# Two feed-forward layers on one core: two output quarters of a Strassen product start from values that ScalarE and VectorE wrote into PSUM, a bank is set aside for one of them, and three gate/up pairs of a layer stay plain, where four did

## The chip, the core and the metric

The kernel runs on 1 core of a Trainium2 chip. The metric is the device time of one execution in microseconds (us). The engines are TensorE (PE, the matrix products; its weight loads are listed apart as PEld), VectorE (DVE), ScalarE (ACT), GpSimd (POOL) and SyncE (SP, which here only issues DMAs). Products go to PSUM, which has 8 banks of 512 fp32 values in each of 128 partitions; everything else lies in SBUF.

## What is computed

Two layers on x of 512 tokens by 1024 channels. Layer 0 mixes the tokens by dilated attention, layer 1 by pooling over windows. After each mixer comes a feed-forward block with 2816 hidden channels, and a norm stands before each part. The change touches the feed-forward blocks alone.

```python
D_MODEL = 1024; SEQ = 512; D_FF = 2816

def swiglu_ffn(h, w_gate_up, w_down):
    gu = h @ w_gate_up
    gate, up = gu[..., :D_FF], gu[..., D_FF:]
    return (jax.nn.silu(gate) * up) @ w_down

def reference(...):
    for i in range(DEPTH):                      # 2
        x = x + mixer_i(rmsnorm(x, norm_i), ...)
        x = x + swiglu_ffn(rmsnorm(x, ffn_norm[i]), w_ffn_gate_up[i], w_ffn_down[i])
    return rmsnorm(x, final_norm)
```

## The kernel before

**Layout and precision.** x lies in SBUF as 8 tiles `X[0..7]` of 128 channels by 512 tokens. Every fp32 operand is split into a high and a low part (`split`, L92: ACT rounds the value, DVE subtracts, L96). A product step is three matmuls, high by high, high by low and low by high (L328, L329, L331 in `Product.add`; L461 to L463 in `mult`).

**The feed-forward block (`ffn`, L1096).** The 2816 hidden channels are 22 blocks of 128. For a block j a *pair* is computed: 128 channels of the gate and the same 128 of the up matrix.

- A *plain pair* (`plain_pair`, L1103) is two products of 8 steps each, so 2 x 8 x 3 = 48 matmuls of 128x512. DVE multiplies the gate's and the up's bank by the norm's row (L1106, L1112), ACT applies Silu (L1113), DVE multiplies both (L1114).
- A *Strassen pair* (`strassen_pair`, L1184, over `chained`, L521) treats gate and up as the two halves of a 2x2 block product (halves of the tokens, halves of the 1024 channels). It takes 7 products of 4 steps, 7 x 4 x 3 = 84 matmuls of 128x256. The weights of such a pair come as four tiles, "b", "s", "m" of 1024 columns and a "half" of 512, after two adds on DVE (L192, L193).

Pairs j < NPLAIN = 4 are plain, and during them the operands of the Strassen form are made: `prepare(k)` (L1118), called for k = 0..3, one in each plain pair. One call is 2 DVE operations of L583, then L587, L588, L590 and four splits (three by L96, one with a changed sign by L100).

**One `chained` call.** Three banks, alpha, beta and gamma. In the order of TensorE: "11" into alpha, "1" into gamma, "2" added to alpha, "21" into beta, "3" added to alpha, "22" added to gamma, "4" added to alpha. ACT copies alpha after "11" (a, L537), gamma after "1" (d, L541), alpha after "2" (b, L545) and after "3" (c, L553). DVE gives the output's quarters: beta + a (L549), d - c (L554), b - gamma (L558). The sums a, b, c, d lie in SBUF.

**The order of a feed-forward block.** `PARTS` is 2, 8, 8 and 4 hidden blocks. The loop at L1239 first computes the pairs j < max(2, NPLAIN); then come the 8 *down products* of hidden blocks 0 and 1 (each 2 steps, 6 matmuls of 128x512; L1246 and L1262 to L1267), each read by a DVE add into `X[m]` (`down`, L1234). Below f0 to f7 are these eight products. Then come the Strassen pairs. Hidden blocks 2 to 9 and 10 to 17 go through four more `chained` calls each over down weights (L1249). The last 4 blocks are plain products again.

**Banks.** `ps()` (L82) takes the 8 banks of one pool in turn: a tile takes the bank of the tile eight before it, so its first matmul waits until the readers of that one are done. The output product of the attention, `f` at L1077, is read by the last `residual` add on DVE (L1064); the next thing on TensorE are the products of the first feed-forward pair, which were begun ahead of the norm's row (`begin`, `finish`, L1273).

**What sets the order.** The tile framework schedules the instructions; each engine then runs its own list strictly in order. Weights come through rings (5 tiles of split "w", 4 of "raw"), refilled by `pump`.

## Time and profile before

| what | value |
|---|---|
| median of 3 runs | 1184.02 us (1183.59 to 1184.98) |
| the profiled execution | 1185.19 us, of it a span of 1183.4 us |
| TensorE's granted clock in the profiled execution | 0.999 |
| feed-forward block of layer 0, first product to first Strassen matmul | 465.04 to 520.96 us |
| the same in layer 1, norm's row in use to first Strassen matmul | 862.67 to 902.68 us |

Instructions start in the order of their engine's list. For TensorE the duration in a row is a modelled latency, and the distance from one start to the next is what a matmul costs; for DVE the same distance is used where it ran back to back, since one instruction's last part lies beside the next one's start. Times are counted from the start of the span.

### The profile page before, as it was taken

The numbers are of one execution on the slowest core, as the hardware profiler recorded it, in microseconds if no ns is written. First come the engines' busy times: TensorE is split into PE (matmuls) and PEld (weight loads), VectorE is DVE, ScalarE is ACT, GpSimd is POOL, SyncE is SP. The second block draws the span as 40 slices with busy tenths as digits, with TensorE's granted clock in tenths as the row PEclk, the third lists the DMA queues.
The fourth block names the chain that finished last, engine by engine and source line by source line (L and its number), as shares of the span: only waits on it lengthen the run. The fifth ranks groups of instructions, "written<-read, shape, count | busy, mean of one in ns | idle before, by whom it ended". The sixth has DMA issues, their size and how long they took to land.

```text
span 1183.4 us, 25574 instructions
## 1 busy us (share of the span) xinstructions
PE 1173.5 (99%) x10182; PEld 1122.6 (95%) x10182; DVE 992.7 (84%) x1747; ACT 750.4 (63%) x1341; POOL 174.1 (15%) x169
## 2 busy tenths in 40 slices
PE   9999999999999999999999999999999999999997
PEld 7899999999999989889999999988889999999997
DVE  8987898889789988799988988657789988898875
ACT  8764664656556666757756766776575776676553
POOL 2111111211011002301111111112030111111100
PEclk9999999999999999999999999999999999999999
DMA  8757666665766557957777787798595777777732
GB/s 288 166 125 196 166 164 159 172 156 149 187 159 158 153 159 203 244 109 196 192 194 199 190 202 191 201 260 204 117 203 121 190 199 194 191 196 195 188 90 73
DMA packets 85017, 209.97 MB, mean 177 GB/s; under 512 B 7952, under 2 KB 13216, under 8 KB 84896
## 3 DMA queue, kind: packets, MB, share of 16 engines
q1 hardware_dynamic: 53104, 145.63, 37.3%
q0 software_dynamic: 31504, 62.41, 32.6%
q8 instruction: 80, 1.31, 0.4%
q14 instruction: 41, 0.34, 0.1%
q10 hardware_dynamic: 288, 0.29, 0.1%
HBM read 206.19 MB, written 2.10 MB: 176 GB/s over the span
## 4 chain that ended last, share of the span: by engine, by line
PE 97%; issue 1%; ACT 1%; DVE 1%; POOL 0%; DVEq 0%; POOLq 0%; ACTq 0%
PE ps L461 21%; PE ps L463 21%; PE ps L462 21%; PE ps L328 7%; PE ps L331 7%; PE ps L329 7%; PE ps L637 2%; PE ps L852 2%; PE ps L638 2%; PE ps L639 2%; PE ps L943 2%; PE ps L730 1%; PE ps L749 1%; ACT w L93 0%; PE ps L914 0%
## 5 line engine op out<-in xcount | busy, mean ns | idle before, releaser
L93 ACT ACTIVATE w<-raw 128x1024 fp32r<-128x1024 f32 x271 | 286.5, 1062 | 150.3 <-PE ps L463 78.8
L96 DVE TENSOR_TENSOR w<-raw,w 128x1024 fp32r<-128x1024 f32 x271 | 330.6, 1223 | 47.7 <-ACT w L93 43.4
L461 PE MATMUL ps<-far,w 128*128 128x256 f32 x896 | 246.5, 275 | 0.0
L462 PE MATMUL ps<-far,w 128*128 128x256 f32 x896 | 246.5, 275 | 0.0
L463 PE MATMUL ps<-far,w 128*128 128x256 f32 x896 | 246.4, 275 | 0.0
L461 PE MATMUL ps<-near,w 128*128 128x256 f32 x749 | 210.9, 282 | 0.0
L463 PE MATMUL ps<-near,w 128*128 128x256 f32 x749 | 207.1, 276 | 0.0
L462 PE MATMUL ps<-near,w 128*128 128x256 f32 x749 | 207.0, 276 | 0.0
L462 PEld LDWEIGHTS ps<-far,w 128*128 128x128 f32 x896 | 168.2, 188 | 0.1
L461 PEld LDWEIGHTS ps<-far,w 128*128 128x128 f32 x896 | 168.2, 188 | 0.1
L463 PEld LDWEIGHTS ps<-far,w 128*128 128x128 f32 x896 | 168.2, 188 | 0.0
L461 PEld LDWEIGHTS ps<-near,w 128*128 128x128 f32 x749 | 140.7, 188 | 0.5
L462 PEld LDWEIGHTS ps<-near,w 128*128 128x128 f32 x749 | 140.8, 188 | 0.0
L463 PEld LDWEIGHTS ps<-near,w 128*128 128x128 f32 x749 | 140.8, 188 | 0.0
L328 PE MATMUL ps<-near,w 128*128 128x512 f32 (+1 forms) x332 | 125.9, 380 | 0.0
L331 PE MATMUL ps<-near,w 128*128 128x512 f32 (+1 forms) x332 | 125.0, 376 | 0.0
L329 PE MATMUL ps<-near,w 128*128 128x512 f32 (+1 forms) x332 | 124.9, 376 | 0.0
L176 POOL DMA_DIRECT2D raw<-w_pair x36 | 43.6, 1210 | 297.0 <-DMA raw<-w_pair 123.7
L331 PEld LDWEIGHTS ps<-near,w 128*128 128x128 f32 x332 | 62.3, 188 | 11.6
L328 PEld LDWEIGHTS ps<-near,w 128*128 128x128 f32 x332 | 62.3, 188 | 11.5 <-ACT near L93 0.4
L329 PEld LDWEIGHTS ps<-near,w 128*128 128x128 f32 x332 | 62.5, 188 | 11.3 <-DVE near L96 0.2
L192 DVE TENSOR_TENSOR raw<-raw 128x512 f32<-128x512 f32 x87 | 59.7, 686 | 11.5 <-issue 9.7
(342 smaller groups left out, 2730.3 us busy)
## 6 DMA issues: line engine op xcount, KB each, us to landing
raw<-w_pair SPq DMA_DIRECT2D x80, 512.0 KB, 5.1
raw<-w_qkp SPq DMA_DIRECT2D x42, 512.0 KB, 4.6
raw<-w_pair POOLq DMA_DIRECT2D x36, 512.0 KB, 7.6
raw<-w_dblock SPq DMA_DIRECT2D x32, 512.0 KB, 4.5
raw<-w_qkp POOLq DMA_DIRECT2D x21, 512.0 KB, 7.9
rawhalf<-w_pair SPq DMA_DIRECT2D x36, 256.0 KB, 5.3
raw<-w_v SPq DMA_DIRECT2D x16, 512.0 KB, 4.2
raw<-w_dblock POOLq DMA_DIRECT2D x16, 512.0 KB, 7.3
```

What stands on the lines that cost most here:

```text
L93: made = nc.scalar.activation(hi, v, AF.Copy)
L96: nc.vector.tensor_tensor(lo, v, hi.bitcast(F32), op=OP.subtract)
L176: nc.gpsimd.dma_start(self.b.rearrange("p (a c) -> p a c", a=2), self.src[:, None, 3 * n:].to_broadcast([P, 2, n]), accum_op=OP.add)
L192: nc.vector.tensor_add(a[:, :n], a[:, :n], b[:, :n])
L328: nc.tensor.matmul(self.p[:, cols], w[0][:, s], mh[:, cols], start=self.done == 0, stop=False)
L329: nc.tensor.matmul(self.p[:, cols], w[0][:, s], ml[:, cols], start=False, stop=False)
L331: nc.tensor.matmul(self.p[:, cols], w[1][:, s], mh[:, cols], start=False, stop=self.done == self.n)
L461: nc.tensor.matmul(dst, w.t[0][:, c], th, start=k == 0 and not on, stop=False, skip_group_check=on)
L462: nc.tensor.matmul(dst, w.t[0][:, c], tl, start=False, stop=False, skip_group_check=on)
L463: nc.tensor.matmul(dst, w.t[1][:, c], th, start=False, stop=k == n - 1, skip_group_check=on)
L637: nc.tensor.matmul(o, mh, wh, start=k == 0, stop=False)
L638: nc.tensor.matmul(o, mh, wl, start=False, stop=False)
```

## The change

- `NPLAIN` goes from 4 to 3. `prepare(0)` and `prepare(1)` both stand in the first plain pair, `prepare(2)` and `prepare(3)` in the second and third.
- The pool of 8 banks is closed where the feed-forward part begins, and two others are opened: `psum7` with 7 banks for `ps()`, and `seeded` with one bank.
- In `chained`, beta is the bank `seeded`. ACT writes its copy of alpha (a) straight into it, and "21" adds to that. DVE writes b - d into gamma's bank, and "22" adds to that. Beta and gamma then hold the finished quarters: ACT's Silu reads them from PSUM in two halves, and in the four `chained` calls over down weights DVE adds them from PSUM to `X[m]`. The DVE add of L549 goes, and the subtraction of L558 becomes the one into gamma.
- The operands T["22"] and B["22"] keep their sign (`split` in place of `split_neg`).
- The first product of layer 0's feed-forward block uses the bank `seeded`.
- A branch for a last pair with blocks, which no entry of `PARTS` reaches, is removed.

The pairs that become Strassen pairs are j = 3 in both layers: 54 `chained` calls in place of 52.

```diff
-NPLAIN = 4
+NPLAIN = 3
...
-    psum = ctx.enter_context(tc.tile_pool(name="psum", bufs=8, space=PSUM))
+    first_banks = ExitStack()
+    banks = [first_banks.enter_context(tc.tile_pool(name="psum", bufs=8, space=PSUM))]
...
-        return psum.tile([P, S], F32, tag="ps", name="ps")
+        return banks[-1].tile([P, S], F32, tag="ps", name="ps")
...
-        alpha, beta, gamma = (ps()[:, :H2] for i in range(3))
-        ab, cd = scratch("first"), scratch("sums")
-        a, b, c, d = ab[:, left], ab[:, right], cd[:, left], cd[:, right]
+        alpha, gamma = (ps()[:, :H2] for i in range(2))
+        beta = seeded[0][:, :H2]
+        bs, cd = scratch("first"), scratch("sums")
+        b, c, d = bs[:, left], cd[:, left], cd[:, right]
...
         mult(alpha, wb, 0, T, "11", n)
-        nc.scalar.copy(a, alpha)
+        nc.scalar.copy(beta, alpha)
...
         nc.scalar.copy(b, alpha)
+        nc.vector.tensor_sub(gamma, b, d)
         behind(2)
-        mult(beta, wb, 1, T, "21", n)
+        mult(beta, wb, 1, T, "21", n, on=True)
         wb.done()
-        nc.vector.tensor_add(one[:, left], beta, a)
...
         mult(gamma, wm, 1, T, "22", n, on=True)
         wm.done()
-        nc.vector.tensor_sub(one[:, right], b, gamma)
...
-        return alpha
+        return beta, gamma, alpha
...
+    first_banks.close()
+    banks.append(ctx.enter_context(tc.tile_pool(name="psum7", bufs=7, space=PSUM)))
+    seeded = [ctx.enter_context(tc.tile_pool(name="seeded", bufs=1, space=PSUM)).tile([P, S], F32, tag="seeded", name="seeded")]
...
                 nc.vector.tensor_mul(gt, pg, row)
-                prepare(j)
+                prepare(j + (j > 0))
+                if j == 0:
+                    prepare(1)
...
-                left = chained(T, gt, u, ftile, K2, inner=True, after=hooks)
-                if not right:
-                    nc.scalar.activation(gt, gt, AF.Silu)
-                    nc.vector.tensor_mul(u[:, H2:], u[:, H2:], gt[:, H2:])
+                beta, gamma, left = chained(T, u, ftile, K2, inner=True, after=hooks)
+                nc.scalar.activation(gt[:, :H2], beta, AF.Silu)
+                nc.scalar.activation(gt[:, H2:], gamma, AF.Silu)
+                nc.vector.tensor_mul(u[:, H2:], u[:, H2:], gt[:, H2:])
...
-                        one, two = ftile("one"), ftile("two")
-                        chained(D, one, two, ftile, (end - first) // 2, after=waiting())
-                        for q, v in ((m, one), (m + 1, two)):
-                            if last and m < KC - 2:
-                                late.append(later(down, q, v, last))
-                            else:
-                                down(q, v, last)
+                        two = ftile("two")
+                        parts = chained(D, two, ftile, (end - first) // 2, after=waiting())
+                        for a, p in enumerate(parts[:2]):
+                            x = X[m][:, a * H2:(a + 1) * H2]
+                            nc.vector.tensor_add(x, x, p)
+                        down(m + 1, two, last)
...
-        lead = begin(2, 1, range(KC - 1))
+        lead = begin(2, 1, range(KC - 1), seeded[0])
```

The lines of the changed kernel that the prediction names: L97 is `split`'s subtraction, L189 and L190 the two adds on raw weights, L535 and L543 ACT's copies, L544 the subtraction into gamma, L552 d - c, L580, L584, L585 and L587 the operations of `prepare`, L1061 the attention's `residual` add, L1107, L1115 and L1117 the multiplications of a plain pair, L1222 the add of `down`.

**TensorE, the start of the first feed-forward product of layer 0.** `ps_6259` is the attention's last output product, `ps_6303` (after: `seeded_6303`) the first gate's. DVE_49 and Activation_49 count finished instructions of DVE and ACT. Before:

```order
L331 MATMUL ps_6259<-near_82,w_6065 128x512
L328 MATMUL ps_6303<-near_82,w_6097 128x512 [waits Activation_49]
L329 MATMUL ps_6303<-near_82,w_6097 128x512
L331 MATMUL ps_6303<-near_82,w_6097 128x512 [waits DMASW3_49]
L328 MATMUL ps_6303<-near_82,w_6097 128x512
```

After:

```order
L328 MATMUL ps_6259<-near_82,w_6065 128x512
L325 MATMUL seeded_6303<-near_82,w_6097 128x512 [waits DVE_49,Activation_49]
L326 MATMUL seeded_6303<-near_82,w_6097 128x512
L328 MATMUL seeded_6303<-near_82,w_6097 128x512 [waits DMASW3_49]
L325 MATMUL seeded_6303<-near_82,w_6097 128x512
```

The first matmul has a wait on DVE that it did not have. The instruction that it waits for is the last L1061 add, the reader of `ps_6259`: the pool's closing waits for all readers of its banks.

**DVE, layer 0, the rows up to the first `down` add.** `far<-temp` and `far<-u` are splits of Strassen operands, `w<-raw` splits of weights, `u<-ps,row` the up product of the last plain pair. Before:

```order
L587 TENSOR_TENSOR temp<-temp 128x2x256
L96 TENSOR_TENSOR far<-temp,far 128x512
L588 TENSOR_TENSOR temp<-temp 128x256
L100 SCALAR_TENSOR_TENSOR far<-temp,far 128x256
L590 SCALAR_TENSOR_TENSOR temp<-temp 128x256
L96 TENSOR_TENSOR w<-raw,w 128x1024
L96 TENSOR_TENSOR far<-temp,far 128x512 x2
L1112 TENSOR_TENSOR u<-ps,row 128x512
L193 TENSOR_TENSOR raw<-raw 128x512
L1114 TENSOR_TENSOR u<-u,gt 128x512
L96 TENSOR_TENSOR far<-u,far 128x256
L1234 TENSOR_TENSOR x<-x,ps 128x512
```

After:

```order
L1115 TENSOR_TENSOR u<-ps,row 128x512
L584 TENSOR_TENSOR temp<-temp 128x2x256
L97 TENSOR_TENSOR far<-temp,far 128x512
L585 TENSOR_TENSOR temp<-temp 128x256
L97 TENSOR_TENSOR far<-temp,far 128x256
L587 SCALAR_TENSOR_TENSOR temp<-temp 128x256
L1117 TENSOR_TENSOR u<-u,gt 128x512
L97 TENSOR_TENSOR far<-temp,far 128x512 x2
L97 TENSOR_TENSOR w<-raw,w 128x1024
L189 TENSOR_TENSOR raw<-raw 128x512
L1222 TENSOR_TENSOR x<-x,ps 128x512
L190 TENSOR_TENSOR raw<-raw 128x512
```

The reader of the last plain pair's up product has moved ahead of the last `prepare`; behind it stand that `prepare`, a weights split and one raw add, and then the first `down` add.

**DVE, layer 1, the reader of the last plain pair's up product.** The names are the same. Before, the third pair's up product had its reader L1112 here (the fourth pair follows):

```order
L587 TENSOR_TENSOR temp<-temp 128x2x256
L96 TENSOR_TENSOR far<-temp,far 128x512
L588 TENSOR_TENSOR temp<-temp 128x256
L100 SCALAR_TENSOR_TENSOR far<-temp,far 128x256
L590 SCALAR_TENSOR_TENSOR temp<-temp 128x256
L1112 TENSOR_TENSOR u<-ps,row 128x512
L96 TENSOR_TENSOR far<-temp,far 128x512
L96 TENSOR_TENSOR w<-raw,w 128x1024
```

After, in the third pair, the last plain one:

```order
L580 SCALAR_TENSOR_TENSOR temp<-x,nrm,row 128x512 x2
L189 TENSOR_TENSOR raw<-raw 128x512
L584 TENSOR_TENSOR temp<-temp 128x2x256
L97 TENSOR_TENSOR far<-temp,far 128x512
L585 TENSOR_TENSOR temp<-temp 128x256
L97 TENSOR_TENSOR far<-temp,far 128x256
L587 SCALAR_TENSOR_TENSOR temp<-temp 128x256
L190 TENSOR_TENSOR raw<-raw 128x512
L97 TENSOR_TENSOR far<-temp,far 128x512 x2
L97 TENSOR_TENSOR w<-raw,w 128x1024
L1115 TENSOR_TENSOR u<-ps,row 128x512
L1222 TENSOR_TENSOR x<-x,ps 128x512
```

The third pair's reader has moved back: before, one weights split stood behind it; now the whole last `prepare`, both raw adds and a weights split stand in front of it, and the first `down` add right behind it.

More of the change, by code (lines that the diff above doesn't have):

```diff
@@ L300, in trunk, with __init__ @@
     class Product:
-        def __init__(self, n, ins, w=None, keep=None):
-            self.n, self.ins, self.done, self.p, self.w = n, ins, 0, ps(), w
+        def __init__(self, n, ins, w=None, keep=None, p=None):
+            self.n, self.ins, self.done, self.p, self.w = n, ins, 0, ps() if p is None else p, w
             self.sizes = units_of(n)
@@ L431, in row_of, with begin @@
         return row
-    def begin(n, layer, ks):
-        return [Product(KC, stream(layer)).add(ks) for i in range(n)]
+    def begin(n, layer, ks, p=None):
+        return [Product(KC, stream(layer), p=None if i else p).add(ks) for i in range(n)]
     def finish(lead, layer, ks):
@@ L519, in seven, with chained @@
         behind(6)
-    def chained(T, one, two, scratch, n, inner=False, after={}):
+    def chained(T, two, scratch, n, inner=False, after={}):
         (unit,), = units.popleft()
         left, right = slice(0, H2), slice(H2, S)
-        alpha, beta, gamma = (ps()[:, :H2] for i in range(3))
-        ab, cd = scratch("first"), scratch("sums")
-        a, b, c, d = ab[:, left], ab[:, right], cd[:, left], cd[:, right]
+        alpha, gamma = (ps()[:, :H2] for i in range(2))
+        beta = seeded[0][:, :H2]
+        bs, cd = scratch("first"), scratch("sums")
+        b, c, d = bs[:, left], cd[:, left], cd[:, right]
         def behind(i):
@@ L1133, in prepare @@
                 n = tuple(T["n"][:, e, k % 2 * H2:(k % 2 + 1) * H2] for e in range(2))
-                split_neg(*n, b22)
+                split(*n, b22)
                 T["22", k] = n
@@ L1182, in waiting, with strassen_pair @@
                 return hooks
-            def strassen_pair(u, first=None, right=None):
+            def strassen_pair(u):
                 gt = ftile("gt")
@@ L1211, in gate_up @@
                     plain_pair(j, u)
-                elif block and odd and j == FC - 1:
-                    strassen_pair(u, later(operands, i, U["even"]), later(operands_right, i, u))
                 else:
```

16 lines of the change are left out of this document (1 added, 15 removed).

## The prediction

> **What bounds the kernel now.** I read the page's busy times and its chain first. Columns of the first row: busy us, share of the span, instructions.
>
> ```profile
> PE 1173.5 (99%) x10182; PEld 1122.6 (95%) x10182; DVE 992.7 (84%) x1747; ACT 750.4 (63%) x1341; POOL 174.1 (15%) x169
> ...
> PE 97%; issue 1%; ACT 1%; DVE 1%; POOL 0%; DVEq 0%; POOLq 0%; ACTq 0%
> ```
>
> TensorE bounds nearly the whole span, so a matmul saved is time saved unless TensorE waits somewhere instead. What one costs comes from the timeline around the first Strassen matmul of layer 0 and of layer 1 (columns: start us, modelled duration, engine, line).
>
> ```profile
> 520.28 0.39 PE L328 MATMUL ps<-near,w 128*128 128x512 f32 x1
> 520.50 0.39 PE L329 MATMUL ps<-near,w 128*128 128x512 f32 x1
> 520.73 0.39 PE L331 MATMUL ps<-near,w 128*128 128x512 f32 x1
> 520.96 0.28 PE L461 MATMUL ps<-far,w 128*128 128x256 f32 x1
> 521.07 0.28 PE L462 MATMUL ps<-far,w 128*128 128x256 f32 x1
> 521.19 0.28 PE L463 MATMUL ps<-far,w 128*128 128x256 f32 x1
> ...
> 902.68 0.28 PE L461 MATMUL ps<-far,w 128*128 128x256 f32 x1
> ```
>
> From start to start a 128x512 matmul takes 0.227 us and a 128x256 one 0.113. Next I asked where another engine has no room left: the busy times by stretch (columns: length, then PE, PEld, DVE, ACT, POOL busy, granted clock, DMA share, GB/s).
>
> ```profile
> 481.00:503.00 22.00, 22.00 (x98) 18.20 (x98) 21.97 (x39) 17.12 (x25) 6.98 (x7) 1.00 1.04 222
> 503.00:513.50 10.50, 10.50 (x48) 8.67 (x48) 10.50 (x19) 5.77 (x10) 0.36 (x1) 1.00 0.60 118
> 513.50:523.00 9.50, 9.50 (x52) 8.22 (x51) 9.24 (x15) 3.11 (x5) 1.20 (x1) 1.00 0.60 112
> 560.00:598.00 38.00, 38.00 (x338) 38.00 (x337) 34.87 (x65) 26.85 (x49) 4.85 (x4) 1.00 0.74 194
> ```
>
> While the plain pairs and the down products of layer 0 run, DVE is as full as TensorE: 32.47 of 32.50 us between 481 and 513.5. It makes the Strassen operands there. In the later stretch it has 8% to spare. A change that brings TensorE to the end of the first stage earlier meets a DVE that cannot follow.
>
> **The change part by part.**
>
> *Fewer matmuls.* A plain pair is 48 x 0.2267 = 10.88 us, a Strassen pair 84 x 0.1133 = 9.52. Two layers: 2 x 1.36 = **2.72 us less** on the bounding engine.
>
> *The closing of the pool.* Before, the first feed-forward matmul follows the attention's last output product at once:
>
> ```profile
> 464.81 0.39 PE L331 MATMUL ps<-near,w 128*128 128x512 f32 x1
> 465.04 0.39 PE L328 MATMUL ps<-near,w 128*128 128x512 f32 x1
> ...
> 465.49 0.69 DVE L383 TENSOR_TENSOR sq<-sq 128x512 f32<-128x512 f32 x1
> 466.09 0.68 DVE L1064 TENSOR_TENSOR x<-x,ps 128x512 f32<-128x512 f32 x1
> ```
>
> Now it waits, as the order shows, for the L1061 add that reads that product. DVE, busy with L383 until then, gets to it at 466.09 and ends at 466.77. TensorE has nothing else in its list: everything behind is queued, the norm's statistics among it, so that DVE's stage starts as much later and the delay stays. **1.7 us more** (466.77 - 465.04). It would be nothing only if that add ran a whole 1.7 us earlier, and nothing ahead of it in DVE's list has gone.
>
> *Seven banks in layer 0.* DVE starts its full stage when the norm's row is there:
>
> ```profile
> 480.95 0.69 DVE L1106 TENSOR_TENSOR gt<-ps,row 128x512 f32<-128x512 f32 x1 [4.26 <-ACT row L430]
> ...
> 498.63 0.42 DVE L588 TENSOR_TENSOR temp<-temp 128x256 f32<-128x256 f32 x1
> 498.96 0.42 DVE L100 SCALAR_TENSOR_TENSOR far<-temp,far 128x256 fp32r<-128x256 f32 x1
> 499.30 0.42 DVE L590 SCALAR_TENSOR_TENSOR temp<-temp 128x256 f32<-128x256 f32 x1
> 499.63 0.68 DVE L1112 TENSOR_TENSOR u<-ps,row 128x512 f32<-128x512 f32 x1
> 500.23 0.68 DVE L96 TENSOR_TENSOR far<-temp,far 128x512 fp32r<-128x512 f32 x1
> 500.83 1.22 DVE L96 TENSOR_TENSOR w<-raw,w 128x1024 fp32r<-128x1024 f32 x1
> 501.97 0.69 DVE L96 TENSOR_TENSOR far<-temp,far 128x512 fp32r<-128x512 f32 x1
> 502.57 0.69 DVE L1114 TENSOR_TENSOR u<-u,gt 128x512 f32<-128x512 f32 x1
> 503.17 1.41 DVE L583 SCALAR_TENSOR_TENSOR temp<-x,nrm,row 128x512 f32<-128x512 f32 x2
> 504.49 0.69 DVE L192 TENSOR_TENSOR raw<-raw 128x512 f32<-128x512 f32 x1
> ...
> 510.28 0.69 DVE L1112 TENSOR_TENSOR u<-ps,row 128x512 f32<-128x512 f32 x1
> ...
> 512.42 0.68 DVE L1234 TENSOR_TENSOR x<-x,ps 128x512 f32<-128x512 f32 x1
> ```
>
> Start to start, back to back: 0.60 us for an operation of 512, 0.335 for 256, 0.66 for one of L583 (1.32 for two), 1.14 for a weights split. In the changed order of DVE there stand, from the row's first use to the first `down` add, 28 operations of 512, 8 of L580, 12 of 256 and 2 weights splits: 16.8 + 5.28 + 4.02 + 2.28 = 28.4 us. So that add starts at 480.95 + 28.4 = 509.35 and ends, 0.69 later, at 510.05, in the clock of before (the 1.7 us above moves both sides). The same sum for the order before (32, 8, 13 and 2) gives 31.1 us, and 31.47 were measured (512.42 - 480.95), so it runs up to 0.3 short.
>
> TensorE's side: before, the 48 down matmuls end at 520.96, so they begin at 510.08; without a fourth plain pair at 499.20. With 7 banks in turn, f7 takes the bank of f0, and the first `down` add frees it. f7 is due 42 matmuls after f0's start, at 499.20 + 9.52 = 508.72. Wait: 510.05 - 508.72 = 1.3, with the 0.3 above 1.6; **I take 1.4 us more**. With 8 banks, f7 took the bank of the fourth pair's up product, which L1112 had freed at 510.97, 8.6 us ahead of f7's turn at 519.60.
>
> *Seven banks in layer 1.* DVE's order differs there. f6 takes the bank of the third pair's up product, whose reader L1115 now stands behind the last `prepare`, both raw adds and three weights splits in all.
>
> ```profile
> 862.67 0.69 DVE L1106 TENSOR_TENSOR gt<-ps,row 128x512 f32<-128x512 f32 x1 [4.20 <-ACT row L430]
> ...
> 894.14 0.68 DVE L1234 TENSOR_TENSOR x<-x,ps 128x512 f32<-128x512 f32 x1
> ```
>
> 27 operations of 512, 8 of L580, 12 of 256, 3 weights splits: 16.2 + 5.28 + 4.02 + 3.42 = 28.9. L1115 starts at 891.6 and ends at 892.3. The down products begin at 902.68 - 10.88 - 10.88 = 880.92, and f6 is due 36 matmuls later, at 889.08. **3.2 us more.** f0's bank is free 0.6 us after that, ahead of f7's turn 1.36 us after f6's.
>
> *The seeds.* "22" now waits for DVE's L544, and "21" for ACT's copy into beta. No row of before has ACT write PSUM; DVE does so once (L516).
>
> ```profile
> L545 ACT COPY first<-ps 128x256 f32<-128x256 f32 x52 | 19.1, 368 | 32.6 <-PE ps L463 32.6
> L516 DVE TENSOR_TENSOR ps<-ps,sums 128x512 f32<-128x512 f32 x21 | 14.6, 693 | 0.0
> L502 DVE TENSOR_TENSOR qk<-ps,first 128x512 f32<-128x512 f32 x21 | 14.4, 686 | 0.0
> ```
>
> L516 writes 512 values to PSUM in 693 ns, L502 writes as many to SBUF in 686, so I price L544 like any 256 operation of DVE (0.42) and the copy at the 0.37 of L545; no row excludes that ACT's is cheaper or dearer, and as the copy has a whole product's time (1.36) to itself, neither would show. In a `chained` call "2" ends 3 x 1.36 = 4.08 us after the start, ACT's copy b 0.37 later, L544 0.42 after that: 4.87. "22" is due at 5 x 1.36 = 6.80, so 1.9 us are to spare, 0.8 where a weights split (1.14) has just begun on DVE. Nothing, then, in 53 of 54 calls. The exception is the first call of layer 0, where the down adds hold DVE up: from the first of them 9 operations of 512 and 3 weights splits, 8.8 us, stand ahead of L544, which ends at 509.35 + 8.8 + 0.4 = 518.6. f7 ends 1.36 after 510.1, and "22" is due 6.80 later, at 518.3: **0.3 us more**. In layer 1 two weights splits stand there (7.7 us): done at 900.4, due at 892.3 + 2.72 + 6.80 = 901.8, nothing.
>
> *The rest, at nothing.* The DVE add that goes (0.33 a call), Silu in two halves (on ACT 2 x 0.42 for 0.62), the unsigned splits and the adds from PSUM lie under TensorE, which the 560 to 598 row shows full while DVE has 3.1 us and ACT 11 us free. If that cover went, 54 x 0.33 would be gained on DVE and 38 x 0.2 lost on ACT.
>
> *Sum.* -2.72 + 1.7 + 1.4 + 3.2 + 0.3 = +3.9 us. Against the profiled execution, 1185.19, that is 1189.1; it was 1.17 above the median of the runs, so I give the median: 1184.02 + 3.9 = **1187.9 us**. If every unknown fell well (sums exact, no 0.3) it is 1187.5, if DVE's sums run 0.3 short in both layers 1188.4.
>
> A rule speaks against the change here. The row first: f7's bank had been free for 8.6 us with 8 banks, and is late with 7. The Trainium skill, Perfetto Trace Analysis, section Matmul Optimizations, asks to use all 8 banks for parallel work, and its section Optimizing Tensor Performance wants groups of matmuls to rotate through banks so that reading one lies beside filling the next. It gives no price; without the rule's effect the sum would lack its 1.4 and 3.2 and stand at -0.7. No run here yet shows seven.
>
> **The rivals.**
>
> *Faster: DVE gets there in time.* The point is the two readers: if the first `down` add of layer 0 ends by 508.72 and L1115 of layer 1 by 889.08, and the closing of the pool costs nothing since only the one bank's own reader counts, all three terms go and 1184.02 - 2.72 = 1181.3 remains. For it: the operations that stand ahead of these readers are partly for later pairs. Against it: DVE's list is strict, it is 100% busy from 480.95 on, and the sum of the order before came within 0.4 us of the measured one. Chance 0.05.
>
> *Within 0.2%: some terms are not there.* With the closing alone, -2.72 + 1.7 gives 1183.0; with layer 0's wait and the late L544 as well 1184.7; with layer 1's wait in place of layer 0's two, 1186.2. It takes an error of mine in which bank follows which, or in DVE's list. Chance 0.16.
>
> *Much slower: the seed of gamma is late in every call.* If in a usual pair not one but two weights splits stand between b and L544, it ends 2.28 - 1.9 = 0.4 us late, in 54 calls 20 us: 1208. For it: DVE is 92% busy in that stretch (34.87 of 38). Against it: L544 stands in the lists of nearly all pairs ahead of the splits. Chance 0.07.
>
> *Slower still by the clock.* A wait of 3.2 us is longer than any that TensorE has in the profile before:
>
> ```profile
> PE ps L914 <- DVE idle L911: 1.2, 1, 1.2
> ```
>
> So no row shows what follows such a gap. If the clock were halved behind it while the last two down products run, their 12 matmuls would take 12 x 0.227 = 2.7 us more: 1190.6. The Trainium skill, TensorE: Matmul & The Clock Gate, part on the HAM clock gate, states this as a rule: an idle window of about 3.4 us puts TensorE at half clock until it has been busy for as long. Every stretch quoted above has a granted clock of 1.00. Chance 0.09.
>
> *The change doesn't do what it says.* The order shows that it does (two DVE operations fewer and one seed a call, 54 calls), so it gets no chance of its own.
>
> **How the numbers follow.** Forecast 0.63, faster 0.05, some terms missing 0.16, late seeds 0.07, clock 0.09. About 0.2% (2.4 us, so 1181.6 to 1186.4) is what a measurement of this kernel can tell from no change. Faster by more: 0.05. Within: 0.16. Slower: 0.63 + 0.07 + 0.09 = 0.79. The range runs from 1184.7, which takes in the upper part of the missing terms, to 1190.8, which takes in the clock; it leaves out the faster case, the late seeds and the other half of the missing terms, 0.2.
>
> **What would show it right or wrong.** In the profile after, TensorE should have a wait of 1.7 us ahead of the first feed-forward product of layer 0, ended by L1061; one of 1.3 to 1.6 some 42 matmuls into its down products, ended by the first L1222; a short one ahead of the first "22", by L544; and one of 3.2 to 3.5 ahead of f6 in layer 1, ended by L1115. From the first Strassen pair of a layer to its end there should be no wait, at 0.113 us a matmul. It is wrong if the down products run through without gaps, if L544 releases TensorE in pair after pair, or if the granted clock falls.

## The result: 0.8% slower, and the profile after

The changed kernel takes 1193.85 us (median of 4 runs, 1193.04 to 1194.20), the one before 1184.5 (4 runs): ratio 1.0081, 95% interval 1.0068 to 1.0093, or 9.4 us more. Forecast were 3.9 more. The profiled execution took 1194.02 us with a span of 1192.2, 8.8 longer than before.

The page and its chain first, as for the kernel before:

```profile
PE 1175.2 (99%) x10254; PEld 1124.9 (94%) x10254; DVE 986.4 (83%) x1725; ACT 748.6 (63%) x1387; POOL 170.7 (14%) x165
...
PE 89%; DVE 6%; issue 2%; DMA 1%; ACT 1%; POOL 0%; DVEq 0%; POOLq 0%; ACTq 0%; SPq 0%
```

The 72 matmuls more are the exchange of two plain pairs for two Strassen pairs (2 x 84 - 2 x 48). TensorE's share of the chain has fallen from 97% to 89%, and 6% of it now is DVE. Whom TensorE waited for (columns: waiter, releaser, us in total, times, longest):

```profile
PE ps L325 <- DVE u L1115: 3.0, 1, 3.0
PE seeded L325 <- DVE x L1061: 1.7, 1, 1.7
PE ps L421 <- POOL rcol L414: 1.5, 1, 1.5
PE ps L325 <- DVE x L1222: 1.3, 1, 1.3
PE ps L911 <- DVE idle L908: 1.2, 1, 1.2
```

Three of the four forecast waits stand there nearly to the size (3.0, 1.7 and 1.3 us, for 3.2, 1.7 and 1.4). The fourth, 0.3 us for L544, did not come, and the one for `rcol` on POOL was not forecast. Where the rest went shows when the two kernels are laid stage by stage beside each other. The table takes the start of TensorE's first matmul of each stage in the two traces; "count" is what 48 matmuls of 512 less (10.88 us) or 84 of 256 more (9.52) do to a stage by themselves.

| stage, from the first matmul of one to that of the next | before us | after us | count | left over |
|---|---|---|---|---|
| up to the attention's last plain products | 459.54 | 459.76 | 0 | +0.2 |
| last attention products and first feed-forward products, to the norm's statistics | 16.47 | 18.49 | 0 | **+2.0** |
| statistics, norm's row | 4.03 | 6.05 | 0 | **+2.0** |
| layer 0, plain pairs and down products, to the first Strassen matmul | 40.92 | 31.65 | -10.88 | **+1.6** |
| layer 0, Strassen stretch | 247.74 | 258.98 | +9.52 | **+1.7** |
| last plain part, pooling mixer, norm | 93.06 | 93.16 | 0 | +0.1 |
| layer 1, plain pairs and down products | 40.92 | 34.91 | -10.88 | **+4.9** |
| layer 1, Strassen stretch | 247.56 | 257.19 | +9.52 | +0.1 |
| last part, to the end of the span | 33.19 | 32.06 | 0 | -1.1 |

The left-overs sum to 11.5, less 2.7 of count: 8.8. (The last row's 1.1 us is no work: TensorE's last matmuls take as long in both, and the last output lands sooner.) Three of the rows are dearer than forecast by something that was not in the sum: the norm's row, layer 1's plain pairs and down products, and layer 0's Strassen stretch.

**The norm's row, +2.0.** POOL's timeline around the statistics of layer 0, in the kernel before (columns: start, duration, engine, line):

```profile
476.77 1.39 POOL L417 TENSOR_TENSOR rcol<-var,nhalf 128x2 f32<-128x2 f32 x2 [7.06 <-DVE var L414]
478.86 2.66 POOL L152 DMA_DIRECT2D w<-w_pair  x3 [0.70 <-ACT w L150]
484.59 1.21 POOL L176 DMA_DIRECT2D raw<-w_pair  x1 [3.06 <-DMA raw<-w_pair]
```

The same in the changed kernel:

```profile
481.14 1.21 POOL L173 DMA_DIRECT2D raw<-w_pair  x1 [11.20 <-issue]
481.89 1.89 POOL L414 TENSOR_TENSOR rcol<-var,nhalf 128x2 f32<-128x2 f32 x2
483.22 2.31 POOL L149 DMA_DIRECT2D w<-w_pair  x2
```

With a plain pair less, the first Strassen pair's accumulating DMA (L173) has moved ahead of the norm's power (L414) in POOL's list. It adds onto a tile that SP loads first, and that load, issued at 466.54, took 13.9 us to land where the median is 4.5. (The profile puts POOL's wait down to "issue" and not to this load. But POOL's semaphore wait for this DMA lasts 11.4 us, from 469.1 to 480.5, and the load landed at 480.4.) The changed kernel's busy times by stretch show DMA full there (the last column but one is its share):

```profile
465.00:470.00 5.00, 3.27 (x15) 2.37 (x14) 3.45 (x6) 3.46 (x5) 1.52 (x3) 1.00 1.09 230
470.00:475.00 5.00, 5.00 (x24) 4.14 (x23) 0.00 (x0) 0.00 (x0) 0.00 (x0) 1.00 1.11 255
```

POOL stood still for 11.2 us; `var` was there at 478.93, and the power began at 481.89. DVE's first multiplication then came at 485.21, 6.3 us behind `var`, and not 4.3.

**Layer 1, +4.9.** The reader of f6's bank came where the sum had put it: DVE's stage began at 869.00, and L1115 stands 29.1 us later.

```profile
869.00 0.69 DVE L1107 TENSOR_TENSOR gt<-ps,row 128x512 f32<-128x512 f32 x1 [4.20 <-ACT row L427]
...
896.93 1.23 DVE L97 TENSOR_TENSOR w<-raw,w 128x1024 fp32r<-128x1024 f32 x1
898.08 0.68 DVE L1115 TENSOR_TENSOR u<-ps,row 128x512 f32<-128x512 f32 x1
898.68 0.68 DVE L1222 TENSOR_TENSOR x<-x,ps 128x512 f32<-128x512 f32 x1
```

But after this wait TensorE ran at half speed for some 3 us (columns: length, PE, PEld, DVE, ACT, POOL busy, granted clock, DMA share, GB/s):

```profile
896.00:898.00 2.00, 0.00 (x0) 0.00 (x0) 2.00 (x3) 1.85 (x2) 0.06 (x1) 1.00 0.06 25
898.00:899.00 1.00, 0.19 (x1) 0.19 (x2) 1.00 (x3) 0.00 (x0) 1.00 (x1) 0.63 0.00 0
899.00:901.00 2.00, 2.00 (x5) 1.61 (x6) 2.00 (x4) 0.42 (x1) 0.14 (x1) 0.50 0.86 147
901.00:902.00 1.00, 1.00 (x4) 0.76 (x4) 1.00 (x2) 0.00 (x0) 0.00 (x0) 0.67 0.83 244
902.00:904.00 2.00, 2.00 (x14) 1.78 (x14) 2.00 (x5) 0.76 (x1) 0.00 (x0) 1.00 1.11 206
```

From 899.4 to 901.5 the matmuls of f6 and f7 start 0.427 us apart, for 0.227. From the start of f6 at 898.81 to the first Strassen matmul at 902.99 the 12 matmuls take 4.18 us, for 2.72. That is 1.5 us: the case of the clock, which the prediction had as a rival, at a little over half its price. The other 3.4 of the 4.9 are the late bank.

**Layer 0, Strassen stretch, +1.7.** The first call, for which 0.3 us had been forecast, runs without a wait. The loss lies in the second to the fifth call, in four short waits for ACT's copies: at 528.1 and 538.0 for L535, at 551.0 and 560.9 for L543. In front of the first two copies stand splits of weights, of the other two splits of Strassen operands, and these splits had waited for DVE or for a DMA. ACT ahead of the copy of 538:

```profile
536.33 1.07 ACT L94 ACTIVATE w<-raw 128x1024 fp32r<-128x1024 f32 x1 [1.08 <-DMA raw<-w_pair]
537.30 0.37 ACT L1194 ACTIVATE gt<-ps 128x256 f32<-128x256 f32 x1
537.56 0.63 ACT L94 ACTIVATE half<-rawhalf 128x512 fp32r<-128x512 f32 x1
538.08 0.38 ACT L535 COPY seeded<-ps 128x256 f32<-128x256 f32 x1
```

### The profile page after: what moved, and what is told of

Same layout as the page of the kernel before. It is cut to its first block, busy times and chain, and to the rows that moved or that the text cites. A ratio compares the mean times of both kernels' runs of the same rounds, so it can differ in the third digit from the quotient of the medians.

```text
span 1192.2 us, 25750 instructions
## 1 busy us (share of the span) xinstructions
PE 1175.2 (99%) x10254; PEld 1124.9 (94%) x10254; DVE 986.4 (83%) x1725; ACT 748.6 (63%) x1387; POOL 170.7 (14%) x165
## 4 chain that ended last, share of the span: by engine, by line
PE 89%; DVE 6%; issue 2%; DMA 1%; ACT 1%; POOL 0%; DVEq 0%; POOLq 0%; ACTq 0%; SPq 0%
PE ps L458 19%; PE ps L459 19%; PE ps L460 19%; PE ps L325 4%; PE ps L326 4%; PE ps L328 4%; PE ps L849 2%; PE ps L634 2%; PE ps L635 2%; PE ps L636 2%; PE seeded L458 2%; PE seeded L459 2%; PE seeded L460 2%; PE ps L940 2%; DVE far L97 1%
## 5 line engine op out<-in xcount | busy, mean ns | idle before, releaser
L97 DVE TENSOR_TENSOR w<-raw,w 128x1024 fp32r<-128x1024 f32 x277 | 335.1, 1223 | 64.7 <-ACT w L94 62.4
L94 ACT ACTIVATE w<-raw 128x1024 fp32r<-128x1024 f32 x277 | 290.6, 1063 | 144.0 <-PE ps L460 52.1
L458 PE MATMUL ps<-far,w 128*128 128x256 f32 x776 | 213.8, 276 | 0.4 <-ACT seeded L535 0.2
L459 PE MATMUL ps<-far,w 128*128 128x256 f32 x776 | 213.5, 275 | 0.0
L460 PE MATMUL ps<-far,w 128*128 128x256 f32 x776 | 213.5, 275 | 0.0
L458 PE MATMUL ps<-near,w 128*128 128x256 f32 x701 | 197.7, 282 | 0.0
L460 PE MATMUL ps<-near,w 128*128 128x256 f32 x701 | 193.9, 277 | 0.0
L459 PE MATMUL ps<-near,w 128*128 128x256 f32 x701 | 193.8, 276 | 0.0
L458 PEld LDWEIGHTS ps<-far,w 128*128 128x128 f32 x776 | 145.6, 188 | 1.2 <-ACT seeded L535 0.7
L459 PEld LDWEIGHTS ps<-far,w 128*128 128x128 f32 x776 | 145.7, 188 | 0.1
L460 PEld LDWEIGHTS ps<-far,w 128*128 128x128 f32 x776 | 145.7, 188 | 0.0
L458 PEld LDWEIGHTS ps<-near,w 128*128 128x128 f32 x701 | 131.7, 188 | 0.5
L459 PEld LDWEIGHTS ps<-near,w 128*128 128x128 f32 x701 | 131.8, 188 | 0.0
L460 PEld LDWEIGHTS ps<-near,w 128*128 128x128 f32 x701 | 131.8, 188 | 0.0
L325 PE MATMUL ps<-near,w 128*128 128x512 f32 (+1 forms) x292 | 110.8, 382 | 4.4 <-DVE u L1115 3.0
L326 PE MATMUL ps<-near,w 128*128 128x512 f32 (+1 forms) x292 | 110.0, 377 | 0.0
L328 PE MATMUL ps<-near,w 128*128 128x512 f32 (+1 forms) x292 | 109.8, 376 | 0.0
L173 POOL DMA_DIRECT2D raw<-w_pair x38 | 45.8, 1205 | 329.3 <-ACT w L94 92.1
L325 PEld LDWEIGHTS ps<-near,w 128*128 128x128 f32 x292 | 55.1, 189 | 15.1 <-DVE u L1115 3.5
L189 DVE TENSOR_TENSOR raw<-raw 128x512 f32<-128x512 f32 x89 | 61.0, 686 | 8.9 <-issue 6.2
L326 PEld LDWEIGHTS ps<-near,w 128*128 128x128 f32 x292 | 55.3, 189 | 10.3 <-DVE near L97 0.7
L328 PEld LDWEIGHTS ps<-near,w 128*128 128x128 f32 x292 | 55.1, 189 | 10.2
```

The costliest lines, as they stand in the source:

```text
L94: made = nc.scalar.activation(hi, v, AF.Copy)
L97: nc.vector.tensor_tensor(lo, v, hi.bitcast(F32), op=OP.subtract)
L173: nc.gpsimd.dma_start(self.b.rearrange("p (a c) -> p a c", a=2), self.src[:, None, 3 * n:].to_broadcast([P, 2, n]), accum_op=OP.add)
L189: nc.vector.tensor_add(a[:, :n], a[:, :n], b[:, :n])
L325: nc.tensor.matmul(self.p[:, cols], w[0][:, s], mh[:, cols], start=self.done == 0, stop=False)
L326: nc.tensor.matmul(self.p[:, cols], w[0][:, s], ml[:, cols], start=False, stop=False)
```

## The experiments

Theory A: the cost is a set of waits at single places (the closing, POOL, late banks, the clock), and the seeds cost nothing. Theory B, its rival, changes with the run. Every experiment was timed in 5 rounds against the kernel before on the same chip; its median there was 1183.9 to 1184.3. Left-overs are those of the table above, from the profile of each run. A profile is one execution: those of e6, e11 and e12 lie 1.5, 2.2 and 3.6 us above the median of their runs, that of e1 2.4 below, so differences of that size between two profiles need not come from the edit.

| run | median us | ratio (95%) | to statistics | row | layer 0 plain, down | layer 0 Strassen | layer 1 plain, down | layer 1 Strassen |
|---|---|---|---|---|---|---|---|---|
| changed kernel | 1193.85 | 1.0081 (1.0068, 1.0093) | +2.0 | +2.0 | +1.6 | +1.7 | +4.9 | +0.1 |
| e1 three plain pairs only | 1195.47 | 1.0098 (1.0082, 1.0113) | 0 | +4.4 | +1.2 | +3.2 | +2.2 | +1.5 |
| e2 four plain, seeded | 1186.51 | 1.0024 (1.0013, 1.0036) | +2.0 | 0 | 0 | -0.1 | 0 | 0 |
| e3 held bank | 1196.89 | 1.0109 (1.0093, 1.0124) | 0 | +5.6 | +2.5 | +2.5 | +5.1 | +0.7 |
| e4 power ahead | 1191.40 | 1.0061 (1.0047, 1.0075) | +2.0 | 0 | +1.6 | +1.4 | +5.1 | +0.5 |
| e5 held bank, power ahead | 1189.77 | 1.0050 (1.0037, 1.0062) | 0 | 0 | +1.6 | +1.7 | +5.0 | +0.1 |
| e6 late bank, power ahead | 1186.63 | 1.0027 (1.0015, 1.0039) | 0 | 0 | +0.1 | +2.7 | +2.2 | +2.0 |
| e7 the same, copy first | 1187.10 | 1.0026 (1.0015, 1.0037) | 0 | 0 | +0.1 | +2.7 | +2.2 | +0.7 |
| e8 late bank, four plain | 1184.75 | 1.0005 (0.9996, 1.0014) | 0 | 0 | 0 | -0.1 | 0 | 0 |
| e9 e5 with a busy wait | 1187.74 | 1.0039 (1.0026, 1.0053) | 0 | 0 | +1.6 | +1.7 | +3.6 | +0.1 |
| e10 e6 without a DMA | 1185.63 | 1.0008 (0.9999, 1.0018) | 0 | 0 | +0.1 | +2.4 | +2.2 | +0.1 |
| e11 e6, up product first | 1187.38 | 1.0026 (1.0011, 1.0041) | 0 | 0 | +0.2 | +5.1 | +2.0 | +1.2 |
| e12 e11, down adds first | 1193.84 | 1.0077 (1.0059, 1.0095) | 0 | 0 | +0.2 | +9.4 | +0.2 | +6.7 |

### e1: three plain pairs and nothing else

The kernel before with

```diff
-NPLAIN = 4
+NPLAIN = 3
...
-                prepare(j)
+                prepare(j + (j > 0))
+                if j == 0:
+                    prepare(1)
```

> The kernel before with three plain pairs a layer (prepare(0) and prepare(1) in the first) and nothing else: 8 banks, no seeds. Theory A (waits at places, read from the two traces): 2.7 us fewer matmuls; the accumulating DMA of the first Strassen pair still stands ahead of the norm's power on POOL, so 2.0 back; no closing, no wait in layer 0's down products; 1.9 in layer 1 at the eighth down product, short of what halves the clock; up to 1.7 in the first Strassen pairs of layer 0. Sum +2.9 against before, about 1187.4. Theory B (the seeds and the 7 banks cost it all): 2.7 faster than before, about 1181.8.

Neither came: 1195.5, 11.6 us above before. Theory B is gone, since without seeds, with 8 banks and no closing, the kernel is as slow as the changed one. Theory A had the places right and the sizes wrong. The accumulating DMA stands ahead of the power here too (so the count alone moves it), and TensorE, which comes 2 us earlier without the closing, waits for it longer. Its list of waits:

```profile
PE ps L424 <- POOL rcol L417: 3.5, 1, 3.5
PE ps L328 <- DVE u L1114: 1.7, 1, 1.7
PE ps L461 <- ACT first L537: 1.5, 3, 1.1
```

The granted clock is 0.50 from 483 to 486 behind that wait, and stays 1.00 behind the one of 1.7 us in layer 1.

### e2: the changed kernel with four plain pairs

```diff
-NPLAIN = 3
+NPLAIN = 4
...
-                prepare(j + (j > 0))
-                if j == 0:
-                    prepare(1)
+                prepare(j)
```

> The changed kernel with four plain pairs again: seeds, closing and 7 banks stay. Theory A: only the closing's 2.0 us remain; no wait in the down products (their banks' readers are done 7 us ahead), the norm's power is ahead of the DMA on POOL again, granted clock 1.00 all through: about 1186.5. Theory B (each seeded call costs): nearly the whole 12 us that the change lost on top of its 2.7 of gain remain, about 1194 to 1196.

1186.51, as theory A had it. In the list of waits, one of the feed-forward blocks is left, the closing's:

```profile
PE seeded L325 <- DVE x L1061: 1.7, 1, 1.7
```

### e3: no closing

```diff
-    first_banks.close()
-    banks.append(ctx.enter_context(tc.tile_pool(name="psum7", bufs=7, space=PSUM)))
-    seeded = [ctx.enter_context(tc.tile_pool(name="seeded", bufs=1, space=PSUM)).tile([P, S], F32, tag="seeded", name="seeded")]
+    seeded = [ps()]
```

> The changed kernel without closing the pool: the seeded bank is one tile of the pool of 8, held to the end, and the first product takes another bank. Theory A: the wait of 1.9 us ahead of the first feed-forward product goes and everything shifts with it, 2.0 less than the changed kernel, about 1191.8; the other waits stay. Theory B: DVE's stage, not TensorE, sets the time of that part, so the wait comes back further on: no change, about 1193.8.

Both missed. The wait for L1061 is gone, and the kernel is not faster: 1196.9. In its place TensorE waits 4.5 us for the power, behind a DMA that POOL could issue at 481.47, 0.3 later than in the changed kernel:

```profile
PE ps L420 <- POOL rcol L413: 4.5, 1, 4.5
PE ps L324 <- DVE u L1112: 3.1, 1, 3.1
```

And the longer wait costs the clock, which the shorter one had not. Busy times by stretch, with the granted clock third from the end:

```profile
479.00:481.00 2.00, 0.00 (x0) 0.00 (x0) 0.00 (x0) 0.00 (x0) 0.00 (x0) 1.00 0.93 375
481.00:483.00 2.00, 0.00 (x0) 0.00 (x0) 0.00 (x0) 0.00 (x0) 1.53 (x3) 0.59 0.10 41
483.00:486.00 3.00, 2.51 (x10) 2.42 (x11) 0.00 (x0) 0.40 (x1) 2.86 (x4) 0.50 0.80 105
```

So the two left-overs of 2.0 in the changed kernel were no sum: the second wait ends when a DMA lands, and the first one lay inside it.

### e4: the norm's power ahead of the DMA

The changed kernel with one edge of order on POOL:

```diff
-            nc.gpsimd.dma_start(self.b.rearrange("p (a c) -> p a c", a=2),
-                                self.src[:, None, 3 * n:].to_broadcast([P, 2, n]), accum_op=OP.add)
+            made = nc.gpsimd.dma_start(self.b.rearrange("p (a c) -> p a c", a=2),
+                                       self.src[:, None, 3 * n:].to_broadcast([P, 2, n]), accum_op=OP.add)
+            if pin_adds:
+                tc.keep_in_program_order(made)
...
                 nc.vector.tensor_mul(gt, pg, row)
+                pin_adds.clear()
...
+        pin_adds.append(True)
         lead = begin(2, 1, range(KC - 1), seeded[0])
```

> The changed kernel with one edge more: the accumulating DMA of the first Strassen pair is issued on POOL behind the norm's power. Theory A: the wait of 1.5 to 1.7 us for rcol goes and DVE's stage starts 2.0 earlier, 2.0 less, about 1191.8. Theory B: the weights of the first Strassen pairs come later by it, and what is won there is lost again in the first pairs of layer 0: about 1193 to 1194.

Theory A: 1191.4. The row's stage is back at 4.03 us, the stages behind it are what they were, and the first Strassen pairs lose no more than without the edge (+1.4 for +1.7). POOL's timeline:

```profile
478.22 1.38 POOL L416 TENSOR_TENSOR rcol<-var,nhalf 128x2 f32<-128x2 f32 x2 [9.04 <-DVE var L413]
480.32 1.78 POOL L149 DMA_DIRECT2D w<-w_pair  x2 [0.71 <-ACT w L147]
481.43 1.90 POOL L173 DMA_DIRECT2D raw<-w_pair  x1
```

### e5: both edits

> Both edits at once: the seeded bank held out of the pool of 8 (no closing) and the accumulating DMA behind the norm's power. Theory A: alone, the first gained nothing because the norm's power waited on POOL for a DMA that lands at about 481 whatever TensorE does; with that out of the way the closing's 2.0 us come off the 1191.4 of the power alone, 1189.4, up to 0.8 more where the first Strassen weights are late. Theory B: holding the bank costs something by itself: no gain over 1191.4.

1189.77: with the power ahead, the closing's share shows (to statistics 16.47, as before), 1.6 of the 2.0 in the medians. Theory A.

### e6: the seeded bank taken late

As e5, but the first product is an ordinary tile of the pool, and the seeded bank is drawn where a layer's Strassen pairs begin, so that plain pairs and down products have 8:

```diff
-    seeded = [ps()]
+    seeded = []
...
             def gate_up(j, ahead):
+                if j == NPLAIN:
+                    seeded[:] = [ps()]
```

> The same, and the seeded bank is taken from the pool only where the Strassen pairs of a layer begin, so that the plain pairs and the eight down products rotate through 8 banks. Theory A: the wait of 1.6 in layer 0 goes, the one of 3.2 in layer 1 shrinks to 1.9 and with it the half clock (1.7) goes: 4.6 less than the kernel with both edits, about 1184.8, up to 1 us more where the weights of the first Strassen pairs are late. Theory B (DVE, not the banks, sets the time of this stage): the waits move to the first Strassen pair and at most 1.5 is won, about 1188.

1186.63, between the two, nearer to A. The down products of layer 0 run without a gap (+0.1), the wait of layer 1 is 1.7 us and the clock behind it stays 1.00: 4.3 us less in these two stages, close to the 4.6 of theory A. But the Strassen stretches lose 2.8 more than in e5, part of it in waits for ACT's copies (L544 1.0 us, L536 0.7 in two) and for DVE's L545 (0.3). This profile lies 1.5 above its median, so the usual loss is smaller: from e5 to e6 the stages give 1.5 less, the medians 3.1 less.

### e7: ACT's copy first

```diff
-        nc.scalar.copy(beta, alpha)
+        with tc.high_priority():
+            nc.scalar.copy(beta, alpha)
```

> The late bank and the power ahead, and ACT's copy into beta (and what hangs on it) is scheduled ahead of splits of weights. Theory A: the waits of the first Strassen pairs of layer 0 (1.7 us in the changed kernel) come from that copy standing behind splits of weights that have not landed; they shrink by 0.5 to 1.5. Theory B: the weights themselves are late, and TensorE waits for them instead: no change.

No change in the median (1187.1 against 1186.6) nor in layer 0 (+2.7); in layer 1 the stretch lost 0.7, and not 2.0, a difference no larger than what e6's profile lies above its median. That is theory B's time. ACT's timeline in layer 0 shows why moving one copy does little (line 93 is the split of weights, 537 the copy):

```profile
530.34 1.07 ACT L93 ACTIVATE w<-raw 128x1024 fp32r<-128x1024 f32 x1 [1.78 <-DMA raw<-w_pair]
531.31 0.36 ACT L1195 ACTIVATE gt<-ps 128x256 f32<-128x256 f32 x1
531.57 0.62 ACT L93 ACTIVATE half<-rawhalf 128x512 fp32r<-128x512 f32 x1
532.09 0.40 ACT L93 ACTIVATE near<-u 128x256 fp32r<-128x256 f32 x1
532.39 0.37 ACT L537 COPY ps<-ps 128x256 f32<-128x256 f32 x1
```

The copy still stands behind a split of weights that waits for its DMA.

### e8: the seeds alone

e6's bank and seeds with four plain pairs (NPLAIN and `prepare` as in e2, no edge on POOL).

> Four plain pairs, the seeds, and the seeded bank taken late from the pool of 8: the seeds without the count, the closing and the 7 banks. Theory A: the seeds cost and bring nothing, within 0.5 us of the kernel before (1184.0). Theory B (each of 52 calls costs, 0.03 or more): 1.5 or more above it; and were DVE's dropped add worth something, below it.

1184.75, ratio 1.0005 (0.9996 to 1.0014), which is 0.6 us with an interval from -0.5 to 1.7: the seeds and the drawn bank cost nothing that these runs tell from no change, and the add that they save brings nothing. In the profile no feed-forward stage differs from before by more than 0.1. Theory A, though the 0.8 between the medians is more than its 0.5.

### e9: matmuls inside the wait

e5 with 12 more matmuls that nobody reads, ahead of f6 in layer 1:

```diff
+                    if layer and not last and m == 6:
+                        for i in range(12):
+                            tc.keep_in_program_order(nc.tensor.matmul(seeded[0], act[0][0][:, :P], act[0][0], start=True, stop=True))
```

> The kernel of both edits (held bank, power ahead) with 12 matmuls of 128x512 more in layer 1, ahead of f6, into the held bank, which nobody reads there: they take 2.7 us and run inside the wait of 3.1. Theory A (the clock is halved because TensorE was idle for 3 us): the granted clock stays 1.00, f6 and f7 run at 0.227 us a matmul, and 12 matmuls more make the kernel 1.6 us faster than the 1189.8 without them, about 1188.2. Theory B (the slow matmuls come from something else at that place): the rate of f6 and f7 stays at 0.43, and the time is 1189.8 or, where the matmuls run over the wait, up to 1 more.

1187.74, 2.0 less than e5 with more work; in the profiles 1.5 of it lie in this stage (+3.6 for +5.0), what the half clock had cost in the changed kernel. The wait for L1115 has shrunk to 0.4, and the clock stays full (busy times by stretch):

```profile
890.00:892.00 2.00, 2.00 (x10) 1.68 (x9) 2.00 (x5) 1.94 (x4) 0.00 (x0) 1.00 0.34 131
892.00:893.00 1.00, 1.00 (x6) 0.75 (x4) 1.00 (x2) 0.72 (x1) 0.52 (x1) 1.00 0.00 0
893.00:894.00 1.00, 0.64 (x3) 0.30 (x2) 1.00 (x3) 0.00 (x0) 0.68 (x1) 1.00 0.00 0
894.00:896.00 2.00, 2.00 (x10) 1.63 (x9) 2.00 (x5) 0.42 (x1) 0.00 (x0) 1.00 0.81 139
```

So idleness halves the clock there, nothing else at that place. The Trainium skill, TensorE: Matmul & The Clock Gate, part on the HAM clock gate, names idleness as the cause too, with an idle window of about 3.4 us. The half clock of the changed kernel lasts as long (by the rows above from 898.3 to 901.7), but the wait that led to it was shorter, 3.0 us, as in e3, e4 and e5 (3.1), and here the measurement decides. Behind waits of 1.3 to 2.1 us (the changed kernel, e1, e6, e11) there was no drop.

### e10: without the accumulating DMA

```diff
+            if no_sum:
+                return
             made = nc.gpsimd.dma_start(self.b.rearrange("p (a c) -> p a c", a=2),
```

> The late-bank kernel without the accumulating DMA of the Strassen weights from the first feed-forward layer on, so that the tiles s and m lack one block of the weights; everything else as it is. What TensorE computes is as much, only its data change. Theory A (the waits of 2.7 us in the first Strassen pairs of layer 0 and 1.8 in layer 1 come from weights that land late through two DMAs in a row): they shrink to under 0.5 each, 1186.6 - 3.5 = about 1183. Theory B (they come from what DVE and ACT have left to do at that place): no change, within 0.7 of 1186.6.

1185.63, between the two. Layer 1's stretch is whole (+0.1 for +2.0), layer 0's is not (+2.4 for +2.7). In layer 0 most of the lateness did not come through this DMA. In layer 1 it may have: the medians differ by 1.0, but e7 had only +0.7 there with the DMA in place, so that a part of the 2.0 belongs to that one execution of e6.

### e11 and e12: the readers first

```diff
-                nc.vector.tensor_mul(up, pu, row)
+                with tc.high_priority():
+                    nc.vector.tensor_mul(up, pu, row)
```

and in e12 also

```diff
-                    down(m, f.p, last)
+                    with tc.high_priority():
+                        down(m, f.p, last)
```

> The late-bank kernel with the multiplication of the up product by the row scheduled ahead of other DVE work, so that the eighth down product of layer 1 finds its bank free (its reader ends near 881.7 in the clock of before, for 890.4). Theory A (DVE has more to do before the first Strassen pair than the time there holds): the wait of 1.7 only moves, to the first matmul of the first Strassen pair, whose bank the first down add frees; within 0.7 us of 1186.6. Theory B (only the order of that one reader is at fault): 1.7 less, about 1184.9.

> The same, and the eight down adds are scheduled ahead too, so that no bank is late; behind them on DVE stand the last Strassen operands and the splits of weights. Theory A: TensorE then waits for those operands and weights in the first Strassen pair, and DVE now and then for a down product; no gain over 1186.6, up to 2 us more. Theory B: without a late bank the stage holds, the 2.7 us of the count come through but for the late weights, 1183 to 1185.

1187.4 and 1193.8: no gain in either, as theory A had it, but e12 lost 7.2 where it allowed 2. In e11 the wait only changes its place in layer 1 (to the first Strassen matmul, for L1225, the first down add). In e12 no bank is late (+0.2 in both plain stages), and the Strassen stretches lose 9.4 and 6.7 us. TensorE waits there for ACT's copies and splits of weights:

```profile
PE ps L459 <- ACT ps L536: 5.2, 3, 3.3
PE ps L459 <- ACT w L93: 3.6, 4, 1.4
```

In both, late DMAs have a part in it. e11's profiled execution has 2.4 us more in layer 0's Strassen stretch than e6: there a split of weights waited 3.2 us for its DMA, until 533.6. In e12 the longest wait, 3.3 us until 529.8, was for a copy behind a split that had waited 3.8 us for its DMA, and the clock was halved for the 3.4 us behind it.

## Why the prediction was wrong

The sign was right, the size not: +9.4 for +3.9. By its own steps:

- *Fewer matmuls, -2.72.* Right: with four plain pairs in e2 and e8, and with three elsewhere, the stages without waits agree with the pitch of 0.227 and 0.113 (layer 1's Strassen stretch in the changed kernel, 257.19 for 247.56 + 9.52).
- *The closing, +1.7.* Right in place and size: 1.7 in the list of waits, 2.0 in the stage, 2.0 in e2. But e3 shows that taking it away alone gains nothing, as long as the power on POOL waits for a DMA.
- *"So that DVE's stage starts as much later".* **This step failed.** The prediction shifted the norm's row by the closing's 1.7 and took the rest of its chain as it was; no term looked at POOL's list. The change had moved the first Strassen pair's DMA ahead of the norm's power, and the row came 2.0 us later still (e4: 2.4 in the medians).
- *Seven banks in layer 0, +1.4; in layer 1, +3.2.* Right: waits of 1.3 and 3.0, by the readers named, and 1.6 in the stage of layer 0. e6 takes the seven banks away there and with them the 1.6, and in layer 1 the 3.0 falls to 1.7, so that only 1.3 of it was the seventh bank's and 1.7 would stand with eight.
- *The clock.* **Left out of the sum, and this failed too.** It was a rival with a chance of 0.09, though the sum's own wait of 3.2 us was its condition. It came in every one of the profiles with a wait of 3 us or more, in the changed kernel at 1.5 for the 2.7 priced, since the rate was back before f7 was done. e9 shows the cause by taking the idleness away. A falling clock was also among the prediction's own signs of being wrong.
- *The seeds, nothing in 53 of 54 calls, +0.3 in the first of layer 0.* The seeds are free (e8), and no list of waits has the subtraction into gamma above 0.3 us. The 0.3 in the first call did not come. But layer 0's Strassen stretch lost 1.7 in the calls after it: **"nothing in 53 of 54 calls" failed for these**. The sum had priced DVE alone, and the waits were for ACT, whose copies stand behind splits that come late. Undersized by 1.4.
- *The late seeds and the faster case* did not come.

With what the stages measured in place of the terms, 2.0 for the closing, 1.6 and 3.4 for the late banks (the 4.9 of layer 1 less the clock), 1.7 for the Strassen calls of layer 0, and the two that were missing, 2.0 for POOL and 1.5 for the clock, the sum is 12.2 - 2.7 = +9.5. The medians differ by 9.4. That this fits to 0.1 is in part luck, since the two profiles differ by 8.8: the last part, which the change does not touch, was 1.1 shorter in the second. With POOL's 2.0 alone added to its sum the prediction would have stood at 1189.9, still in its range; it took the clock or the Strassen calls as well to leave it.

The gain of 2.7 did not come in any order that was tried (e6, e7, e11 and e12). The reading that fits is that the plain stage was there to give DVE time for the Strassen operands: with 10.9 us less of it, whichever work was put first (operands, readers of banks, a copy), TensorE waited for another. That is argued and not shown, since late DMAs were among those waits in e11 and e12, and another order might do better. The best of the complete kernels with three plain pairs is 1186.6, and the kernel before, at 1184, stays ahead. It also remains open what makes ACT's splits late in layer 0's first Strassen pairs, which cost 1.7 to 2.7 us: without the accumulating DMA most of it stays (e10), one copy's place in ACT's list does not explain it (e7), and DVE's raw adds, which come late in DVE's list, were not tried alone.

## What to carry to other kernels

Ahead of a change that shortens a stage, look at which engine is full in it, and then at the in-order lists of all queues, POOL's among them: an instruction that waits for a transfer and has moved up by one place holds everything behind it (here the norm's power, by 3.0 us). Two waits in a row don't add up when the second ends at an absolute time (a DMA's landing); taking the first away then buys nothing, and can make the second long enough to cost the clock. A stage that looks like plain work for the bounding engine may be the cover for another engine's preparation, as DVE's 32.47 busy us of 32.50 suggest here.

## What the runs showed of the hardware

- Idle waits of TensorE of 3.0 to 4.5 us (the changed kernel, e1, e3 twice, e4, e5, e12) were each followed by half the clock for the next 3 to 5 us of matmuls, waits of up to 2.1 us (e11) were not. The clock record has the half clock for 3.4 us each time, and for 6.8 behind the wait of 4.5. It set in 2.8 to 4.5 us after the start of the last matmul ahead of the wait, in e1 and e4 only when TensorE was already running again. Filling 2.7 us of a wait of 3.1 with matmuls that nobody reads made the kernel 2.0 us faster.
- Writing 256 values to PSUM cost ACT and DVE nearly what writing them to SBUF did: 362 ns for 365, and 431 for 419. The groups of the changed kernel (the number behind the comma is the mean in ns):

```profile
L543 ACT COPY first<-ps 128x256 f32<-128x256 f32 x54 | 19.7, 365 | 27.2 <-PE ps L460 27.2
L535 ACT COPY seeded<-ps 128x256 f32<-128x256 f32 x54 | 19.5, 362 | 21.1 <-PE ps L460 20.8
...
L544 DVE TENSOR_TENSOR ps<-first,sums 128x256 f32<-128x256 f32 x54 | 23.3, 431 | 16.4 <-ACT first L543 16.2
...
L552 DVE TENSOR_TENSOR two<-sums 128x256 f32<-128x256 f32 x16 | 6.7, 419 | 0.0
```

- A 512 KB load whose median is 4.5 us took 13.9 us to land where the DMA share was 1.1.
